# A retention and pooling block in split single precision: scores of 128 queries by one product of 256 columns, and keys, scores and states ahead of the filler

## The chip, the cores and the metric

The kernel runs on one core of a Trainium2 chip. Its time is the device time of one execution in microseconds (us). TensorE (PE in the profile) multiplies, VectorE (DVE) and ScalarE (ACT) do the elementwise work, SyncE (SP) issues the transfers, and GpSimd (POOL) does next to nothing here.

## What is computed

One layer on 1024 tokens of 1024 channels, float32: a gated feed-forward network (2816 wide), a mixing layer with two branches, retention in 4 heads of 256 and trailing mean pooling, and a second feed-forward network. The change lies in the mixing layer, in two places: where the values v are projected, and in the retention:

```python
def retention(q, k, v):
    ...
    scores = jnp.einsum("bnchd,bnshd->bnhcs", qc, kc) * inner_decay[None, None]
    inner = jnp.einsum("bnhcs,bnshe->bnche", scores, vc)

    def step(state, inp):
        q_i, k_i, v_i = inp
        cross = jnp.einsum("bchd,bhde->bche", q_i * q_decay[None, :, :, None], state)
        new_state = state * chunk_decay[None, :, None, None] + jnp.einsum(
            "bchd,bche->bhde", k_i * k_decay[None, :, :, None], v_i)
        return new_state, cross
    ...
    out = inner + cross.transpose(1, 0, 2, 3, 4)
```

## The kernel before

**Products in three parts.** Each float32 operand is split into a high part in the fast format fp32r and a low part, the rest: ACT casts (`copy`, line 161), DVE subtracts (`tt`, line 162; 165 and 166 with a scale). `mm3` (lines 178 to 183) adds three products in PSUM: high by high (181), high by low (182), low by high (183). So a product waits for ACT at line 181 and for DVE's low part at 182 or 183.

**Order of the work.** The kernel is a list of steps, each with a preparation (loads, splits) and a body (products). A helper called `flow` issues preparations four steps ahead of bodies and drains a queue of other work (`work`) in between. A scheduler then orders each engine's instructions statically, and `with soon():` gives instructions priority. PSUM has six rotating banks and two for sums.

**The values stage** (`values`, about 624 to 670 us in the profile). v = u W is one level of Strassen-Winograd's scheme: seven products of quarter blocks, L11 R11, S2 T2, S1 T1, S4 R22, S3 T3, L12 R21, L22 T4, each in four steps. L and S come from the weights (tiles vL, vS; their splits vL11w, vS1w, vS2w), R and T from the normalised activations (n2R, n2T). `block` builds the weight sums S2, S3 and S1 at lines 1271 to 1273. `nx.work` queues the work that makes an activation block; `end_of` does so as parts of the feed-forward network's sum are done: its `end(4)` queues R21 and T4. Just ahead of the values lies the end of that network: products bp6b of bp4m and bp4w, then the sums bd.

**The retention** (about 1153 to 1330 us). A `Unit` is half the sequence (512 tokens) of one head: 8 units, named by head and half (00, 01, 10 and so on). A unit has two spans of 256 tokens, each of two halves of 128. `scores` multiplies keys by queries: for the first 128 keys of a span against 256 queries (j = 0), for the second against 128 (j = 1), each over two halves of the head's 256 channels; DVE then scales by decay (tile sc) and the result is split (tile sm). `keys` transposes the keys (line 1434, PSUM tile kd00b and so on) and splits them with a scale (kd). `update` multiplies kd by v into a new state (PSUM tile st, tile sf, split into state). `across` multiplies queries by the state and `inner` the scores by v, both into ob. Units follow each other in `retention`; between their parts stand fillers, steps of the pooling branch (px) and of its projection (pu).

Of the kernel before, what the change touches and what calls it, by code (L numbers as in the profile page):

```python
# [15 lines left out]
ADD, SUB, MUL = ALU.add, ALU.subtract, ALU.mult  # L16

P = 128
# [27 lines left out]
SPAN = 2 * P  # L46
# [44 lines left out]
def block_kernel(ctx: ExitStack, tc, x, x_tok, vecs, f1_in, f1_out, w_in, w_v, pool_w, w_ret, w_pool, w_o,  # L91
                 f2_in, f2_out, g_row, rope, decay, consts, out, out_tok):
    nc = tc.nc
    mm = nc.tensor.matmul
# [84 lines left out]
    def mm3(dst, w, m, start, stop):  # L179

        mm(dst, w[0], m[0], start=start, stop=False, skip_group_check=True)  # L181
        mm(dst, w[0], m[1], start=False, stop=False, skip_group_check=True)  # L182
        mm(dst, w[1], m[0], start=False, stop=stop, skip_group_check=True)  # L183

    def parts(m, at=slice(None)):
        return m[:, 0, at], m[:, 1, at]
# [924 lines left out]

    mix = Next("n2", V_MIX, h1)

    def end_of(nx):
        def end(part):
            if part == 4:
                nx.work(nx.r21, nx.t4_)
            else:
                nx.work(*{2: (nx.r11,), 5: (nx.r22, nx.p22), 3: (nx.t2, nx.t1, nx.t3)}[part])

        return end

    end1 = end_of(mix)


    tab, stored = {}, set()
# [115 lines left out]
    def values():  # L1242

        nx, kept, two, p1s = mix, {}, {}, {}

        def fetch(r, *rows):

            for z, (k, o) in enumerate(rows):
                load(half(r, z), w_v[k, :, o * H : (o + 1) * H])
            return half(r, 0), half(r, 1)  # L1250

        def rows(n, k):

            if (n, k // 2) not in two:
                at, o = k // 2 * 2 + (4 if n[2] == "2" else 0), (1 if n[1] == "2" else 0)
                two[n, k // 2] = fetch(raw(f"v{n}{k}"), (at, o), (at + 1, o))
            return two[n, k // 2][k % 2]

        def block(n, k):

            if n[0] == "L":
                return rows(n, k)
            if n in ("S1", "S3"):
                return two.pop((n, k))

            L11 = rows("L11", k)
            if n == "S4":
                tt(L11, rows("L12", k), L11, SUB)
                return L11
            L21, L22 = fetch(tl(f"v{n}{k}"), (k, 1), (k + 4, 1))  # L1270
            tt(L22, L21, L22, ADD)
            tt(L21, L11, L21, SUB)
            tt(L11, L22, L11, SUB)
            two["S1", k], two["S3", k] = L22, L21
            return L11

        bk = {}

        def step(L, R, k, where, start, after):
            w = []  # L1280

            def prep():
                t = weights(block(L, k), f"v{L}w{k}")
                w.extend(flat(t, z) for z in range(2))

            def body():
                if start and k == 0:
                    for i in range(4):
                        bk[where, i] = (sum_bank if where == "b" and i < N_SUM else bank)(f"v{L}{i}")
                m = nx.operand(R, k)  # L1290
                for i in range(4):
                    mm3(bk[where, i], parts(m, slice(i * P, (i + 1) * P)), w, start and k == 0, k == 3)
                    if k == 3:
                        with soon():
                            after(i, bk[where, i])

            return prep, body

        def store(o, j, i, src):
            to = vs[2 * o + j].rearrange("p (h t c) -> p h t c", h=2, t=4)  # L1300
            load(to[:, :, i], src.rearrange("p (h c) -> p h c", h=2))
            if i == 3:
                stored.update(f"v{h}{j}" for h in (2 * o, 2 * o + 1))

        def keep(n, i):
            if i % 2 == 0:
                kept[n, i // 2] = t4(f"v{n}{i}")
            return half(kept[n, i // 2], i % 2)

        def old(n, i):  # L1310
            return half(kept[n, i // 2], i % 2)

        def result(o, j, other=None):
            def after(i, b):
                c = c2(f"vc{o}{j}{i}")
                if other is None:
                    copy(c, b)
                else:
                    tt(c, b, other(i), ADD)
                flow.add(lambda: store(o, j, i, c))  # L1320
                if (o, j, i) == (0, 0, 3):
                    nx.stats(between=nx.blocks("R22", [("tl", N_TL)] * 3, True))

            return after

        def after1(i, b):
            p1s[i] = c2(f"vp1{i}")
            copy(p1s[i], b)

        def after6(i, b):  # L1330
            copy(keep("h", i), b)

        def after5(i, b):
            copy(keep("f", i), b)

        def product(L, R, where, start, f):
            return [step(L, R, k, where, start, f) for k in range(4)]

        yield from product("L11", "R11", "a", True, after1)
        for p in zip(product("S2", "T2", "a", False, after6), product("S1", "T1", "b", True, after5)):  # L1340
            yield from p
        for p in zip(product("S4", "R22", "b", False, result(0, 1, lambda i: old("h", i))),
                     product("S3", "T3", "a", False, result(1, 1, lambda i: old("f", i)))):
            yield from p
        yield from product("L12", "R21", "b", True, result(0, 0, lambda i: p1s.pop(i)))
        yield from product("L22", "T4", "a", False, result(1, 0))
# [99 lines left out]
    class Unit:  # L1446
# [65 lines left out]
        def scores(self):  # L1512

            self.sm = []
            for j in range(2):
                wid = SPAN - j * P
                b = bank(f"s{self.name}{j}")
                for s in range(2):
                    at = s * SPAN + j * P
                    for i in range(2):  # L1520
                        mm3(b[:, s * wid : (s + 1) * wid], parts(self.K[i], slice(at, at + P)),
                            parts(self.Q[i], slice(at, at + wid)), s == 0 and i == 0, i == 1)
                n = 2 * wid
                c = c2(f"sc{self.name}{j}")
                m = sb.tile([P, 2, H], F32R, tag="t4", bufs=N_T4, name=f"sm{self.name}{j}")
                with soon():
                    for s in range(2):
                        at = slice(s * wid, (s + 1) * wid)
                        stt(c[:, at], b[:, at], self.row(8, 2 * s + j), self.dec[:, :wid], MUL, MUL)
                    split(m[:, 0, :n], m[:, 1, :n], c[:, :n])  # L1530
                self.sm.append(m)

# [41 lines left out]
        def across(self, s, state):  # L1574
            b, first = self.into(s)
            for t in range(2):
                at = s * SPAN + t * P
                for i in range(2):
                    mm3(self.cell(b, t), parts(self.Q[i], slice(at, at + P)),
                        parts(state, slice(i * HD, (i + 1) * HD)), first and i == 0 and t == 0, i == 1)  # L1580

        def products(self):
            self.ob = {}
            mid = self.update(0)
            if self.nh == 1:
                self.across(0, self.state)
            else:
                self.state = self.update(1)
            for s in range(2):
                self.inner(s)  # L1590
            self.across(1, mid)

        def outputs(self):
            o = self.O[self.nh] = t4(f"o{self.name}")
# [46 lines left out]
    def retention():  # L1641
        filler = fillers()

        def fill(n=1):
            for _ in range(n):
                f = next(filler, None)
                if f is not None:
                    yield f

        yield units[0].operands, units[0].values  # L1650
        for n, u in enumerate(units):
            after = units[n + 1] if n + 1 < len(units) else None

            def scores(u=u, n=n):
                if u.nh == 1:
                    u.follow(units[n - 1])
                u.scores()

            def rest(u=u, after=after):
                u.products()  # L1660
                if after:
                    after.operands()
                u.outputs()
                if u.nh == 1:
                    u.normalise()

            yield none, scores
            yield none, u.keys
            yield from fill()
            if after:  # L1670
                yield after.loads, lambda after=after: (after.values(), after.turn())
            yield none, rest

            late = u.nh == 0 and n
            if n < 3 or late:
                yield from fill()
            if late:
                yield none, units[n - 1].finish
        yield none, lambda: take(range(6))
        yield from fill(2)  # L1680
        yield none, units[-1].finish
        yield none, lambda: take((6, 7))
        yield from fill(2 * KT)
# [278 lines left out]
```

## Time and profile before

| | |
|---|---|
| median of 3 runs | 2150.41 us (2148.95 to 2151.13) |
| the profiled execution's own time | 2149.24 us |
| its span | 2147.2 us |
| PE busy, share of the span | 2134.6 us, 99% |
| DVE busy | 1871.7 us, 87% |
| ACT busy | 1100.8 us, 51% |

The span is the stretch that the profile shows; the other 2.04 us of the execution lie around it. In a timeline row stand the start, the length, the engine, the line, the operation, the output and the inputs, the shape (for PE the stationary operand, then the moving one), the number of instructions, and in brackets the idle time before it with what ended it. Matmuls are pipelined, so their lengths overlap: what a product takes is the distance from its start to the next one's. A row of the stretches names the busy time of each engine, with the number of its instructions.

### The profile page before, as it was taken

To read this page: it belongs to the slowest core of one execution; us is meant where nothing else is said; L and a number is where in the kernel's file an instruction comes from. 1 tells how busy PE (TensorE), PEld (TensorE's weight loads), DVE (VectorE), ACT (ScalarE), POOL (GpSimd) and SP (SyncE) were. 2 spreads that over 40 slices of the span, in tenths; PEclk is the share of its full clock that TensorE was granted. 3 is DMA by queue.
4 is the path that set the end of the run, shared out by engine and by line. 5 is a ranking of instruction groups with operands and counts; after the bars stand their busy time and mean duration, and the time that the engine had idled before them with its cause. 6 is when DMAs were issued, how large, how long until landed. Compare 5 with 4: busy or idle time off the path is not lost.

```text
span 2147.2 us, 30158 instructions
## 1 busy us (share of the span) xinstructions
PE 2134.6 (99%) x10830; PEld 1812.8 (84%) x10830; DVE 1871.7 (87%) x3344; ACT 1100.8 (51%) x2074; POOL 0.2 (0%) x4
## 2 busy tenths in 40 slices
PE   9999999999999999999999999999999999999998
PEld 7888888888887888888888888888888888888887
DVE  8798888997986799999988788899988988899796
ACT  8544444554653544545457653446644544455454
POOL 0000000000000000000000000000000000000000
PEclk9999999999999999999999999999999999999999
DMA  7232323585542333232337566624123232357542
GB/s 257 75 133 74 138 84 134 196 274 177 180 139 89 108 121 114 107 120 108 123 124 231 172 229 235 230 94 161 65 97 124 85 127 84 132 198 274 196 131 100
DMA packets 116102, 313.61 MB, mean 146 GB/s; under 512 B 12784, under 2 KB 17008, under 8 KB 115952
## 3 DMA queue, kind: packets, MB, share of 16 engines
q1 hardware_dynamic: 115376, 310.63, 41.9%
q8 instruction: 85, 1.39, 0.3%
q10 hardware_dynamic: 576, 1.05, 0.1%
q14 instruction: 65, 0.53, 0.1%
HBM read 220.93 MB, written 90.70 MB: 145 GB/s over the span
## 4 chain that ended last, share of the span: by engine, by line
PE 93%; DVE 4%; DMA 1%; ACT 1%; issue 0%; SPq 0%; DVEq 0%; ACTq 0%
PE c_b L181 2%; PE c_b L182 2%; PE c_b L183 2%; PE a_b L181 2%; PE a_b L182 2%; PE a_b L183 2%; PE c_e L181 2%; PE c_e L182 2%; PE c_e L183 2%; PE a_e L182 2%; PE a_e L181 2%; PE a_e L183 2%; PE a_a L181 1%; PE a_a L182 1%; PE a_a L183 1%; PE c_a L182 1%
## 5 line engine op out<-in xcount | busy, mean ns | idle before, releaser
L182 PE MATMUL c_b<-n3T,c_wS 128*128 128x512 f32 x176 | 68.6, 390 | 0.0
L183 PE MATMUL c_b<-n3T,c_wS 128*128 128x512 f32 x176 | 68.5, 389 | 0.0
L181 PE MATMUL c_b<-n3T,c_wS 128*128 128x512 f32 x176 | 68.2, 390 | 0.0
L181 PE MATMUL a_b<-n1T,a_wS 128*128 128x512 f32 x168 | 65.4, 389 | 0.0
L182 PE MATMUL a_b<-n1T,a_wS 128*128 128x512 f32 x168 | 65.4, 389 | 0.0
L183 PE MATMUL a_b<-n1T,a_wS 128*128 128x512 f32 x168 | 65.3, 389 | 0.0
L181 PE MATMUL a_a<-n1R,a_wL 128*128 128x512 f32 x120 | 46.7, 389 | 0.0
L182 PE MATMUL a_a<-n1R,a_wL 128*128 128x512 f32 x120 | 46.7, 389 | 0.0
L183 PE MATMUL a_a<-n1R,a_wL 128*128 128x512 f32 x120 | 46.7, 389 | 0.0
L182 PE MATMUL c_a<-n3R,c_wL 128*128 128x512 f32 x112 | 43.7, 390 | 0.0
L181 PE MATMUL c_a<-n3R,c_wL 128*128 128x512 f32 x112 | 43.6, 389 | 0.0
L183 PE MATMUL c_a<-n3R,c_wL 128*128 128x512 f32 x112 | 43.6, 389 | 0.0
L183 PEld LDWEIGHTS c_b<-n3T,c_wS 128*128 128x128 f32 x176 | 33.0, 188 | 6.9
L181 PEld LDWEIGHTS c_b<-n3T,c_wS 128*128 128x128 f32 x176 | 33.0, 188 | 6.7
L182 PEld LDWEIGHTS c_b<-n3T,c_wS 128*128 128x128 f32 x176 | 33.0, 188 | 6.6
L162 DVE TENSOR_TENSOR a_wS<-a_S,a_wS 128x512 fp32r<-128x512 f32 x45 | 30.6, 682 | 8.2 <-ACT a_wS L161 8.2
L183 PEld LDWEIGHTS a_b<-n1T,a_wS 128*128 128x128 f32 x168 | 31.5, 188 | 6.6
L181 PEld LDWEIGHTS a_b<-n1T,a_wS 128*128 128x128 f32 x168 | 31.5, 188 | 6.5
L182 PEld LDWEIGHTS a_b<-n1T,a_wS 128*128 128x128 f32 x168 | 31.5, 188 | 6.4
L162 DVE TENSOR_TENSOR c_wS<-c_S,c_wS 128x512 fp32r<-128x512 f32 x46 | 31.3, 682 | 3.7 <-ACT c_wS L161 3.6
L182 PE MATMUL c_e<-n3T,c_wL 128*128 128x512 f32 x88 | 34.5, 392 | 0.0
L181 PE MATMUL c_e<-n3T,c_wL 128*128 128x512 f32 x88 | 34.5, 392 | 0.0
(3378 smaller groups left out, 8145.1 us busy)
## 6 DMA issues: line engine op xcount, KB each, us to landing
c_ra<-in_f_in SPq DMA_DIRECT2D x22, 512.0 KB, 3.7
c_rb<-in_f_in SPq DMA_DIRECT2D x22, 512.0 KB, 3.7
a_ra<-in_f_in SPq DMA_DIRECT2D x21, 512.0 KB, 3.7
a_rb<-in_f_in SPq DMA_DIRECT2D x21, 512.0 KB, 3.7
t<-au SPq DMA_DIRECT2D x11, 512.0 KB, 2.9
b<-ag SPq DMA_DIRECT2D x11, 512.0 KB, 4.1
r<-au SPq DMA_DIRECT2D x11, 512.0 KB, 3.7
bra<-in_f_out SPq DMA_DIRECT2D x11, 512.0 KB, 5.5
```

The source lines that it names most:

```text
L162: tt(lo, src, hi.bitcast(F32), SUB)
L181: mm(dst, w[0], m[0], start=start, stop=False, skip_group_check=True)
L182: mm(dst, w[0], m[1], start=False, stop=False, skip_group_check=True)
L183: mm(dst, w[1], m[0], start=False, stop=stop, skip_group_check=True)
```

## The change

There are four edits. In the scores for j = 1, the high part of the keys is multiplied by the high and the low part of the queries side by side, one product of 256 columns into two halves of a PSUM strip; the low part of the keys by the high part of the queries is added to the first half. ACT copies the second halves out, DVE adds the first, and the decay is applied to that sum. In `retention`, keys come first, then scores, then the states (`updates`), and the filler after them; before it was scores, keys, filler, and the states after that, with the rest. R21 and T4 are queued from `values` at the third pair of steps of S2 T2 and S1 T1. The weight sums of `block` get priority.

```diff
-    def end_of(nx):
-        def end(part):
-            if part == 4:
-                nx.work(nx.r21, nx.t4_)
-            else:
-                nx.work(*{2: (nx.r11,), 5: (nx.r22, nx.p22), 3: (nx.t2, nx.t1, nx.t3)}[part])
-
-        return end
-
-    end1 = end_of(mix)
+    def end1(part):
+        mix.work(*{2: (mix.r11,), 5: (mix.r22, mix.p22), 3: (mix.t2, mix.t1, mix.t3)}.get(part, ()))
...
-            tt(L22, L21, L22, ADD)
-            tt(L21, L11, L21, SUB)
-            tt(L11, L22, L11, SUB)
+            with soon():
+                tt(L22, L21, L22, ADD)
+                tt(L21, L11, L21, SUB)
+                tt(L11, L22, L11, SUB)
...
-        for p in zip(product("S2", "T2", "a", False, after6), product("S1", "T1", "b", True, after5)):
+        for k, p in enumerate(zip(product("S2", "T2", "a", False, after6), product("S1", "T1", "b", True, after5))):
+            if k == 2:
+                nx.work(nx.r21, nx.t4_)
             yield from p
...
-                    at = s * SPAN + j * P
+                    at, to = s * SPAN + j * P, b[:, s * SPAN : (s + 1) * SPAN]
                     for i in range(2):
-                        mm3(b[:, s * wid : (s + 1) * wid], parts(self.K[i], slice(at, at + P)),
-                            parts(self.Q[i], slice(at, at + wid)), s == 0 and i == 0, i == 1)
+                        w, m = parts(self.K[i], slice(at, at + P)), self.Q[i][:, :, at : at + wid]
+                        first, final = s == 0 and i == 0, i == 1
+                        if j == 0:
+                            mm3(to, w, (m[:, 0], m[:, 1]), first, final)
+                        else:
+                            mm(to, w[0], m, start=first, stop=False, skip_group_check=True)
+                            mm(to[:, :P], w[1], m[:, 0], start=False, stop=final, skip_group_check=True)
...
                 with soon():
+                    src = b
+                    if j:
+                        both, src = b.rearrange("p (s z c) -> p s z c", s=2, z=2), c
+                        sums = c[:, :n].rearrange("p (s c) -> p s c", s=2)
+                        copy(sums, both[:, :, 1])
+                        tt(sums, both[:, :, 0], sums, ADD)
                     for s in range(2):
                         at = slice(s * wid, (s + 1) * wid)
-                        stt(c[:, at], b[:, at], self.row(8, 2 * s + j), self.dec[:, :wid], MUL, MUL)
+                        stt(c[:, at], src[:, at], self.row(8, 2 * s + j), self.dec[:, :wid], MUL, MUL)
...
+        def updates(self):
+
+            self.mid = self.update(0)
+            if self.nh == 0:
+                self.state = self.update(1)
+
         def products(self):
             self.ob = {}
-            mid = self.update(0)
             if self.nh == 1:
                 self.across(0, self.state)
-            else:
-                self.state = self.update(1)
             for s in range(2):
                 self.inner(s)
-            self.across(1, mid)
+            self.across(1, self.mid)
...
-            yield none, scores
-            yield none, u.keys
+            yield none, keys
+            yield none, u.scores
+            yield none, u.updates
             yield from fill()
```

The order of the instructions moves in the two stages alone. On DVE, at the end of the feed-forward network, these rows follow each other before; vL11w_5938 is the first weight block of the values, bd the sum that ends the network:

```order
L162 TENSOR_TENSOR bp4w_5909<-bL_5879,bp4w_5909 128x512 [waits DMAHW6_49,PE_49]
L162 TENSOR_TENSOR bp4m_5912<-bT_5882,bp4m_5912 128x512 [waits DMAHW0_49,Activation_49]
L318 SCALAR_TENSOR_TENSOR bacc_4359<-bacc_4359,neg,bacc_4363 128x512 [waits DMAHW1_49]
L318 SCALAR_TENSOR_TENSOR bacc_4360<-bacc_4360,neg,bacc_4364 128x512 [waits DMAHW2_49]
L162 TENSOR_TENSOR vL11w_5938<-vL_5935,vL11w_5938 128x512 [waits DMAHW7_49,Activation_49]
L162 TENSOR_TENSOR n2T_5928<-bacc_4359,n2T_5928 128x512 [waits Activation_49]
L162 TENSOR_TENSOR n2T_5932<-bacc_4360,n2T_5932 128x512 [waits Activation_49]
L318 SCALAR_TENSOR_TENSOR bacc_4361<-bacc_4361,neg,bacc_4365 128x512 [waits DMAHW3_49]
L953 TENSOR_TENSOR bd_6000<-bp6b_4193,brb 128x512 [waits PE_49]
```

In the changed kernel the same place on DVE, from bp4m_5912 on, reads:

```order
L162 TENSOR_TENSOR bp4m_5912<-bT_5882,bp4m_5912 128x512 [waits Activation_49]
L318 SCALAR_TENSOR_TENSOR bacc_4359<-bacc_4359,neg,bacc_4363 128x512
L318 SCALAR_TENSOR_TENSOR bacc_4360<-bacc_4360,neg,bacc_4364 128x512
L953 TENSOR_TENSOR bd_6000<-bp6b_4193,brb 128x512 [waits PE_49]
L953 TENSOR_TENSOR bd_6005<-bp6b_4194,brb 128x512 [waits PE_49]
L953 TENSOR_TENSOR bd_6010<-bp6b_4195,brb 128x512 [waits PE_49]
L953 TENSOR_TENSOR bd_6015<-bp6b_4196,brb 128x512 [waits PE_49]
L1264 TENSOR_TENSOR vS_6173<-vS_6173 128x512 [waits DMAHW6_49,DMAHW5_49,DVE_49]
L162 TENSOR_TENSOR n2T_5928<-bacc_4359,n2T_5928 128x512 [waits Activation_49]
L1265 TENSOR_TENSOR vS_6173<-vL_5976,vS_6173 128x512 [waits DVE_49]
L162 TENSOR_TENSOR n2T_5932<-bacc_4360,n2T_5932 128x512 [waits Activation_49]
L162 TENSOR_TENSOR vL11w_5938<-vL_5935,vL11w_5938 128x512
```

The low part of vL11w_5938 stood three places behind that of bp4m_5912 and ahead of bd; now it stands eleven places behind it, after bd and two weight sums (lines 1264 and 1265). Four more of these sums now stand ahead of bp4m_5912, two of them as far up as the earlier bd.

On PE, in the retention's unit 20, the scores of 128 queries (PSUM tile s_11945) end before like this, and the transposes of the keys and a filler (pu1d) follow:

```order
L183 MATMUL s_11945<-q_11883,k_11889 128x128
L181 MATMUL s_11945<-q_11886,k_11892 128x128
L182 MATMUL s_11945<-q_11886,k_11892 128x128
L183 MATMUL s_11945<-q_11886,k_11892 128x128
L1434 MATMUL kd20b_11969<-cst,k_11687 128x128 [waits DMAHW3_49,PE_49]
L1434 MATMUL kd20b_11969<-cst,k_11687 128x128 [waits DMAHW4_49]
L1434 MATMUL kd20b_11969<-cst,k_11687 128x128 x2
L1434 MATMUL kd20b_11979<-cst,k_11687 128x128 x4
L700 MATMUL pu1d_11771<-po_11269,pu1w_11797 128x512
```

In the changed kernel the transposes stand ahead of all scores, and the same place reads:

```order
L1521 MATMUL s_11957<-q_11867,k_11873 128x256 [waits PE_49]
L1522 MATMUL s_11957<-q_11867,k_11873 128x128
L1521 MATMUL s_11957<-q_11870,k_11876 128x256
L1522 MATMUL s_11957<-q_11870,k_11876 128x128
L1521 MATMUL s_11957<-q_11867,k_11873 128x256
L1522 MATMUL s_11957<-q_11867,k_11873 128x128
L1521 MATMUL s_11957<-q_11870,k_11876 128x256
L1522 MATMUL s_11957<-q_11870,k_11876 128x128
L181 MATMUL st_11979<-v_11807,kd_11919 128x256 [waits Activation_49]
L182 MATMUL st_11979<-v_11807,kd_11919 128x256
L183 MATMUL st_11979<-v_11807,kd_11919 128x256 [waits DVE_49]
```

Where twelve products of 128 columns stood, there are four of 256 and four of 128, and the state's products (st) follow at once, with waits for ACT and DVE on kd. Before, 24 filler products stood between the transposes and the first of them.

On DVE, in unit 00, the low part of the first keys (k_10809) stands before in this place; the rows at 1153, 1160 and 589 belong to the projections that end there:

```order
L1153 TENSOR_TENSOR g2A<-g2b,g2A 128x512 [waits DVE_49,PE_49]
L162 TENSOR_TENSOR q_10806<-q_10556,q_10806 128x512
L1160 TENSOR_TENSOR g2A<-g2A,n2rb 128x512 [waits DVE_49]
L162 TENSOR_TENSOR k_10809<-k_10559,k_10809 128x512 [waits DMAHW0_49]
L1153 TENSOR_TENSOR g3B<-g3e,g3v 128x512 [waits PE_49]
```

In the changed kernel:

```order
L1145 TENSOR_TENSOR g2A<-g2b,g2A 128x512 [waits DVE_49,PE_49]
L166 SCALAR_TENSOR_TENSOR kd_10915<-kd00b_10914,by_10901,kd_10915 128x256 [waits Activation_49]
L1152 TENSOR_TENSOR g2A<-g2A,n2rb 128x512 [waits DVE_49]
L166 SCALAR_TENSOR_TENSOR kd_10915<-kd00b_10914,by_10901,kd_10915 128x256 [waits Activation_49]
L162 TENSOR_TENSOR q_10806<-q_10556,q_10806 128x512
L1145 TENSOR_TENSOR g3B<-g3e,g3v 128x512 [waits PE_49]
L589 TENSOR_TENSOR g3A<-g2x_10815,g3A 128x256 [waits Activation_49]
L1152 TENSOR_TENSOR g3B<-g3B,n2rb 128x512 [waits DVE_49]
L166 SCALAR_TENSOR_TENSOR kd_10925<-kd00b_10924,by_10901,kd_10925 128x256 [waits Activation_49]
L1145 TENSOR_TENSOR g3A<-g3b,g3A 128x512 [waits DVE_49]
L162 TENSOR_TENSOR k_10809<-k_10559,k_10809 128x512 [waits DMAHW0_49]
```

The keys' low part moved behind three kd splits and four steps of the projections.

More of the change, by code (lines that the diff above doesn't have):

```diff
@@ L1652, in retention, with keys @@
             after = units[n + 1] if n + 1 < len(units) else None
-            def scores(u=u, n=n):
+            def keys(u=u, n=n):
                 if u.nh == 1:
                     u.follow(units[n - 1])
-                u.scores()
+                u.keys()
             def rest(u=u, after=after):
```

## The prediction

> **What bounds the kernel now.** I read the page's first and fourth parts, then the waits of the tensor engine, then the groups by shape and the timelines of the two stages that the change touches.
>
> ```profile
> PE 2134.6 (99%) x10830; PEld 1812.8 (84%) x10830; DVE 1871.7 (87%) x3344; ACT 1100.8 (51%) x2074; POOL 0.2 (0%) x4
> PE 93%; DVE 4%; DMA 1%; ACT 1%; issue 0%; SPq 0%; DVEq 0%; ACTq 0%
> ```
>
> The tensor engine (PE) is busy for 2134.6 of the span's 2147.2 us, and the chain that ended last is PE for 93% of its length. So the time changes by what PE no longer has to do, and by waits of PE that come or go. All its waits are few:
>
> ```profile
> engine line waited for: us in total, times, longest us
> PE vL L181 <- ACT vS2w L161: 1.5, 1, 1.5
> PE set L204 <- DVE zero L199: 1.2, 1, 1.2
> PE ob L182 <- DVE state L162: 1.1, 2, 0.8
> PE ob L181 <- ACT state L161: 0.6, 2, 0.5
> ```
>
> The 1.2 us is the start of the kernel and stays. The change can touch the other three: one stall of 1.5 us in the values stage, and 1.1 + 0.6 = 1.7 us in which the retention waits for its state. Whatever else it gains must be PE work that vanishes.
>
> **Scores of 128 queries.** Each of the 8 retention units has 2 spans and 2 key halves, so 32 groups; each group was three products of 128 columns and becomes one of 256 and one of 128. The durations of single products overlap, so I price them by the distance between starts, in one stretch of the stage:
>
> ```profile
> 1283.60 0.28 PE L181 MATMUL s<-q,k 128*128 128x256 f32 x1
> ...
> 1284.31 0.23 PE L181 MATMUL s<-q,k 128*128 128x128 f32 x1
> 1284.37 0.27 PE L182 MATMUL s<-q,k 128*128 128x128 f32 x1
> ...
> 1285.15 0.28 PE L183 MATMUL s<-q,k 128*128 128x128 f32 x1
> ```
>
> From 1283.60 to 1284.31 lie six products of 256: 0.118 us each. From 1284.37 to 1285.15 lie seven of 128: 0.111 each. Half as many columns are hardly cheaper: a group costs 3 x 0.111 = 0.333 before and 0.118 + 0.111 = 0.229 after, 0.104 less, and 32 x 0.104 = 3.3 us less PE work. The new operand reads the high and the low part of the queries as two strips of 128. No row shows a product of two strips; its bounds are 0.118 (one strip of 256, above) and 0.222 (two products of 128). I take 0.118, since the rest of the instruction is that row's; at 0.222 the whole 3.3 is gone.
>
> [...]
>
> Off PE each unit gains an ACT copy and a DVE addition of 256 elements:
>
> ```profile
> L162 DVE TENSOR_TENSOR sm<-sc,sm 128x256 fp32r<-128x256 f32 x8 | 3.3, 416 | 0.2
> L161 ACT CAST sm<-sc 128x256 fp32r<-128x256 f32 x8 | 3.3, 407 | 6.5 <-DVE sc L1529 6.3
> ```
>
> That is 8 x 0.41 = 3.3 us on each. What is late by it are the parts of the 128-query scores, by 0.8 us, which the inner products read only after the states and the filler (in unit 20, below, the filler runs from 1245 past 1249.49). I cost it at nothing. Without that cover it would be 8 x 0.8 = 6.4 us.
>
> **States ahead of the filler.** The state products now follow the scores at once, so the state is split while the filler runs, several us before the cross products that read it. The 1.7 us of state waits go. In exchange the kd operands (keys transposed, scaled by ACT and DVE) are needed without the filler between. In the unit 20 of before:
>
> ```profile
> 1244.26 1.06 PE L1434 MATMUL kd20b<-cst,k 128*128 128x128 f32 x8
> 1247.56 0.48 DVE L166 SCALAR_TENSOR_TENSOR kd<-kd20b,by,kd 128x256 fp32r<-128x256 f32 x1
> 1249.13 0.47 DVE L166 SCALAR_TENSOR_TENSOR kd<-kd20b,by,kd 128x256 fp32r<-128x256 f32 x1
> 1249.49 0.39 PE L701 MATMUL pu1d<-po,pu1w 128*128 128x512 f32 x1
> ```
>
> Its transposes end at 1245.32; the second low part is done at 1248.04, 2.7 us later, the fourth at 1249.60, 4.3 later. Between transposes and states now stand 12 x 0.118 + 4 x 0.229 = 2.3 us of scores; the second low part is read 5 products (0.6) into the states, the fourth 17 products (2.0) in: 2.7 against 2.9 and 4.3 against 4.3. So it just fits where ACT and DVE are as free as here, and they are not everywhere:
>
> ```profile
> core 0: us, PE busy (x) PEld busy (x) DVE busy (x) ACT busy (x) POOL busy (x), PEclk, DMA share, GB/s
> 1150.00:1180.00 30.00, 29.84 (x198) 27.03 (x197) 29.85 (x56) 25.04 (x52) 0.00 (x0) 1.00 0.72 232
> 1270.00:1300.00 30.00, 29.52 (x194) 26.61 (x193) 29.89 (x64) 16.35 (x41) 0.00 (x0) 1.00 0.37 128
> ```
>
> DVE is full from 1150 to 1180, where unit 00 starts, and around unit 30, whose keys it rotates first. In unit 00 three kd splits, and four steps of the sums that stood behind, now come ahead of the first keys' low part:
>
> ```profile
> 1158.46 0.68 DVE L162 TENSOR_TENSOR k<-k,k 128x512 fp32r<-128x512 f32 x1
> 1159.06 0.68 DVE L1153 TENSOR_TENSOR g3B<-g3e,g3v 128x512 f32<-128x512 f32 x1
> ...
> 1164.30 0.86 DVE L166 SCALAR_TENSOR_TENSOR kd<-kd00b,by,kd 128x256 fp32r<-128x256 f32 x2
> 1159.67 0.28 PE L183 MATMUL s<-q,k 128*128 128x256 f32 x1
> ```
>
> Three splits at 0.4 (a pair takes 0.86), three steps of 0.6 (1158.46 to 1159.06) and one of half that make it 3.3 us later: done at 1158.46 + 3.3 + 0.68 = 1162.4. PE is given six pool products of 0.23 (the distance of starts at 512 columns, below) and eight transposes of 0.11 ahead of the score product of 1159.67, 2.3 us, and is there at 1162.0: a wait of 0.4. The second keys' low part follows 1.6 later, behind a split and a step, and PE has 1.1 us of work until it: 0.5 more. That is 0.9, between nothing and 3.3. For the other seven units I take 0.7 together (unit 30 and unit 10, whose kd splits stand behind the casts of values and queries), between nothing and 1.15 each (a pair of casts, below). Retention in sum: -3.3 - 1.7 + 0.9 + 0.7 = -3.4. SP's queue moves too: unit 20's q and k loads stand behind some result writes. None of PE's waits ends on a load, and I put nothing for it.
>
> **The values stage.** The work for the operands R21 and T4 is queued later, and three sums over weight rows are pulled ahead by priority. The stall that they can free:
>
> ```profile
> 653.06 0.39 PE L183 MATMUL vS<-vS1w,n2T 128*128 128x512 f32 x1
> 654.93 1.20 PE L181 MATMUL vL<-vS2w,n2T 128*128 128x512 f32 x4 [1.48 <-ACT vS2w L161]
> 631.30 0.39 PE L181 MATMUL vL<-vL11w,n2R 128*128 128x512 f32 x1
> 631.53 0.39 PE L182 MATMUL vL<-vL11w,n2R 128*128 128x512 f32 x1
> ```
>
> Products of 512 start 0.23 apart, so the gap of 1.87 costs 1.64 us. It goes: the sum that vS2w waits for is one of those pulled ahead. But DVE has no idle time here (16.00 of 16 us, first row), so what is put ahead makes something else late:
>
> ```profile
> 624.00:640.00 16.00, 16.00 (x72) 13.15 (x72) 16.00 (x27) 7.40 (x14) 0.00 (x0) 1.00 0.31 110
> 602.96 0.81 SPq L140 DMA_DIRECT2D vL<-in_w_v  x2
> vL<-in_w_v SPq DMA_DIRECT2D x8, 256.0 KB, 3.0
> 605.24 1.28 DVE L967 TENSOR_TENSOR bacc<-bacc,bd 128x512 f32<-128x512 f32 x2
> 625.80 0.68 DVE L162 TENSOR_TENSOR bp4m<-bT,bp4m 128x512 fp32r<-128x512 f32 x1
> 627.73 0.68 DVE L162 TENSOR_TENSOR vL11w<-vL,vL11w 128x512 fp32r<-128x512 f32 x1
> 630.20 2.48 DVE L953 TENSOR_TENSOR bd<-bp6b,brb 128x512 f32<-128x512 f32 x4
> 628.58 0.39 PE L181 MATMUL bp6b<-bp4m,bp4w 128*128 128x512 f32 x1
> 628.81 0.39 PE L182 MATMUL bp6b<-bp4m,bp4w 128*128 128x512 f32 x1
> ```
>
> DVE reaches the first pulled-up sum at 605.24, but its rows, issued at 602.96 with 3.0 to landing, are there at 605.96: 0.7 lost. Four sums at 0.6 (starts at DVE are 0.60 apart) then stand ahead of bp4m's low part: 2.4 + 0.7 = 3.1 later, done at 625.80 + 3.1 + 0.68 = 629.6, where PE wants it at 628.81: a stall of 0.8. Next in the old order came vL11w's low part at 627.73; in the new one it stands behind the four bd sums, two more weight sums and two n2T splits. The bd sums need the last PE product of bp6b and end by 633.2; four steps of 0.6 follow, so vL11w is done at 633.2 + 2.4 + 0.7 = 636.3. PE, with four high products put ahead, wants it at 631.30 + 0.8 + 4 x 0.23 = 633.0: a stall of 3.3. Behind it DVE's next low parts (one every 0.6 to 2.4 us) serve 2.7 us of PE work each, so no further stall. Sum: 0.8 + 3.3 - 1.64 = +2.5. Bounds: -1.6 if PE finds vL11w in time, +4.0 if the last weight rows land late (0.6) and the second split is late as well (0.7).
>
> **Sum.** -3.4 + 2.5 = -0.9 us against the profiled execution's 2149.24 (span 2147.2 and 2.04 around it): 2148.3. The median shown, 2150.41, is 1.2 above that execution, so 2149.5 is forecast. A measurement of this kernel can tell about 0.2%, 4.3 us, from no change; the forecast lies within it.
>
> **The rivals.**
> *Faster: the values stage does not stall.* If DVE's order costs PE nothing there, all that remains is -3.4 - 1.6 = -5.0, and 2145.4; with no new kd waits -6.6 and 2143.8, the most that the change can bring. For it: the old stall ends on ACT, which has slack, and the early stalls rest on times that I chained over 30 us of DVE. Against: the order of DVE is fixed, and no gap in it was there to absorb 3.1 us. Chance 0.28.
>
> *Slower: states wait for kd.* The state products have lost their cover. If in each unit the kd splits stand behind one pair of casts, PE waits for it eight times:
>
> ```profile
> 1248.92 1.15 ACT L161 CAST q<-q 128x512 fp32r<-128x512 f32 x2
> ```
>
> 8 x 1.15 = 9.2 in place of my 0.7 gives -0.9 + 8.5 = +7.6, 2158.0. It decides from a wait of (4.3 + 0.9 + 0.7) / 8 = 0.75 us a unit. For it: 2.7 against 2.9 leaves no margin, and in unit 20 that pair of casts does stand right beside the kd splits. Against: ACT has half its time free, and the kd splits are now released ahead of the scores' parts, not behind them. Chance 0.19.
>
> *The cheap product is not cheap.* Two strips of 128 cost 0.222 as two products do: the 3.3 us are not won, and the sum is +2.4, 2152.8, still within what counts as the same. [...] Against: the seven rows at 0.111. Chance 0.05.
>
> **How the numbers follow.** The forecast has 0.48. Faster by over 0.2% has 0.28, from the first rival; within 0.2% has 0.48 + 0.05 = 0.53; slower 0.19. The range leaves out the corner of the first rival with no new wait at all, and the upper part of the second: 2144.5 to 2155.0.
>
> **What would show it.** Right: s products of 256 columns in place of 192 of the small ones, their starts 0.12 apart; no PE wait on state; the vL wait on vS2w gone; and a new PE wait on vL11w's low part of about 3 us and one on bp4m's of under 1. Wrong: no wait on vL11w (then faster), waits of the st products on kd in most units (then slower), or two-strip products 0.2 apart.

## The result, and the profile after

The changed kernel is slower: 2156.24 us median against 2150.41, a ratio of 1.0028 (95% interval 1.0017 to 1.0039). The forecast was 2149.5, in a range from 2144.5 to 2155.0. Its profiled execution took 2154.68 us with a span of 2151.8.

The first line of its page's busy times, then the waits of PE that bear on the change. The numbers of a wait are us in total, how often, and the longest:

```profile
PE 2133.0 (99%) x10798; PEld 1810.7 (84%) x10798; DVE 1874.5 (87%) x3352; ACT 1103.4 (51%) x2082; POOL 0.2 (0%) x4
```

```profile
PE vL L182 <- DVE vL11w L162: 4.3, 1, 4.3
PE st L181 <- ACT kd L165: 1.6, 3, 1.1
...
PE bp6b L182 <- DVE bp4m L162: 1.2, 1, 1.2
...
PE vS L182 <- DVE vS1w L162: 0.7, 1, 0.7
...
PE px L181 <- DVE g3A L1145: 0.5, 1, 0.5
...
PE s L183 <- DVE k L162: 0.3, 1, 0.3
```

The waits on vS2w (1.5) and on state (1.7) are gone, as forecast. New ones stand in their place, the largest on vL11w.

Where the time went is read from marks that both kernels share: starts of products before the change's places, between them and after. These are rows of the tiles' view, of before and then of after; the numbers behind the colon are lengths in ns, then the first and last start.

```profile
L181 PE MATMUL bp6b<-bp6m,bp6w x44: 389/389/389, 424.6 to 481.0; 128*128 128x512 f32 x44
L181 PE MATMUL q0a<-n2R,q0wL x8: 389/389/389, 711.3 to 718.8; 128*128 128x512 f32 x8
L181 PE MATMUL g3b<-n2T,g3wS x8: 389/389/389, 1135.7 to 1143.1; 128*128 128x512 f32 x8
L181 PE MATMUL ru0a<-ruR,ru0wL x8: 389/389/389, 1358.6 to 1366.1; 128*128 128x512 f32 x8
```

```profile
L181 PE MATMUL bp6b<-bp6m,bp6w x44: 389/389/390, 424.8 to 481.2; 128*128 128x512 f32 x44
L181 PE MATMUL q0a<-n2R,q0wL x8: 389/390/390, 718.2 to 725.7; 128*128 128x512 f32 x8
L181 PE MATMUL g3b<-n2T,g3wS x8: 389/390/390, 1142.3 to 1149.8; 128*128 128x512 f32 x8
L181 PE MATMUL ru0a<-ruR,ru0wL x8: 389/389/390, 1363.3 to 1370.8; 128*128 128x512 f32 x8
```

From bp6b to q0a, the stretch of the values stage, 286.7 us became 293.4: 6.7 lost, where +2.5 was forecast. From the last g3b to the first ru0a, the retention, 215.5 became 213.5: 2.0 won, where 3.4 was forecast. Together that is 4.7, and the span grew by 4.6. The time outside the span grew by 0.8 (from 2.0 to 2.9), for which no row shows a reason.

PE in the values stage of after:

```profile
628.76 0.39 PE L181 MATMUL bp6b<-bp4m,bp4w 128*128 128x512 f32 x1
630.31 0.50 PE L182 MATMUL bp6b<-bp4m,bp4w 128*128 128x512 f32 x1 [1.16 <-DVE bp4m L162]
...
632.96 1.07 PE L181 MATMUL vL<-vL11w,n2R 128*128 128x512 f32 x4
638.35 0.50 PE L182 MATMUL vL<-vL11w,n2R 128*128 128x512 f32 x1 [4.33 <-DVE vL11w L162]
...
639.74 0.63 PE L182 MATMUL vL<-vL11w,n2R 128*128 128x512 f32 x1
640.17 0.63 PE L183 MATMUL vL<-vL11w,n2R 128*128 128x512 f32 x1
...
650.55 0.61 PE L181 MATMUL vS<-vS1w,n2T 128*128 128x512 f32 x2
651.82 0.50 PE L182 MATMUL vS<-vS1w,n2T 128*128 128x512 f32 x1 [0.66 <-DVE vS1w L162]
```

Behind the long wait the products start 0.43 us apart (639.74 to 640.17), not 0.23. The stretches show why. They are cut at 638.95 and 642.36, where the clock changes; in each row the granted clock (PEclk in the head) stands behind the engines, ahead of the DMA's share.

```profile
core 0: us, PE busy (x) PEld busy (x) DVE busy (x) ACT busy (x) POOL busy (x), PEclk, DMA share, GB/s
635.54:638.95 3.41, 0.60 (x3) 0.51 (x4) 3.41 (x7) 0.00 (x0) 0.00 (x0) 1.00 0.01 2
638.95:642.36 3.41, 3.41 (x10) 2.65 (x9) 3.41 (x7) 1.86 (x4) 0.00 (x0) 0.50 0.00 0
642.36:645.78 3.42, 3.42 (x16) 2.80 (x15) 3.42 (x7) 0.95 (x2) 0.00 (x0) 1.00 0.00 0
```

The clock stood at 0.5 for 3.4 us with PE busy throughout, which loses half of that, 1.7. By the distances of the starts, the stretch's loss adds up: 1.55 - 0.23 = 1.3 at bp4m, 638.35 - 632.96 - 4 x 0.23 = 4.5 at vL11w, 1.7 by the clock, 651.82 - 650.55 - 2 x 0.23 = 0.8 at vS1w, less the old 1.64: 6.7.

DVE in the same stretch of after:

```profile
627.76 0.69 DVE L1264 TENSOR_TENSOR vS<-vS 128x512 f32<-128x512 f32 x1 [0.67 <-DMA vS<-in_w_v]
...
631.50 2.48 DVE L953 TENSOR_TENSOR bd<-bp6b,brb 128x512 f32<-128x512 f32 x4
635.20 0.69 DVE L1264 TENSOR_TENSOR vS<-vS 128x512 f32<-128x512 f32 x1 [1.23 <-DMA vS<-in_w_v]
...
637.61 0.68 DVE L162 TENSOR_TENSOR vL11w<-vL,vL11w 128x512 fp32r<-128x512 f32 x1
```

DVE stood 1.23 us for the rows of the fourth weight block, with vL11w's low part four places behind it: PE stood still behind a weight sum that its own products need only later.

### The profile page after: what moved, and what is told of

Its sections match the earlier page's. It is cut to its first block, busy times and chain, and to the rows that moved or that the text cites. A ratio compares the mean times of both kernels' runs of the same rounds, so it can differ in the third digit from the quotient of the medians.

```text
span 2151.8 us, 30116 instructions
## 1 busy us (share of the span) xinstructions
PE 2133.0 (99%) x10798; PEld 1810.7 (84%) x10798; DVE 1874.5 (87%) x3352; ACT 1103.4 (51%) x2082; POOL 0.2 (0%) x4
## 4 chain that ended last, share of the span: by engine, by line
PE 87%; DVE 8%; DMA 2%; ACT 2%; issue 1%; SPq 0%; DVEq 0%; ACTq 0%
PE c_b L181 2%; PE c_b L182 2%; PE c_b L183 2%; PE a_b L181 2%; PE a_b L182 2%; PE a_b L183 2%; PE c_e L181 2%; PE c_e L182 2%; PE c_e L183 2%; PE a_e L182 2%; PE a_e L181 2%; PE a_e L183 2%; PE a_a L181 1%; PE a_a L182 1%; PE a_a L183 1%; PE c_a L182 1%
```

## The experiments

Times are medians; each ratio is to runs of the kernel before on the same chip, whose median was 2149.53 to 2150.41 us. The stretches are read as above, in the one profiled execution of each kernel.

| kernel | us | ratio to before (95%) | values | retention |
|---|---|---|---|---|
| before | 2150.41 | | 286.7 | 215.5 |
| changed | 2156.24 | 1.0028 (1.0017 to 1.0039) | 293.4 | 213.5 |
| values_undone | 2148.48 | 0.9994 (0.9985 to 1.0003) | 286.7 | 214.4 |
| no_soon | 2146.18 | 0.9987 (0.9978 to 0.9995) | 285.0 | 213.1 |
| soon3 | 2151.62 | 1.0009 (1.0000 to 1.0018) | 289.0 | 214.0 |
| filled | 2155.87 | 1.0025 (1.0015 to 1.0035) | 291.8 | 215.9 |
| scores_only | 2146.11 | 0.9983 (0.9974 to 0.9992) | 286.8 | 211.6 |
| order_only | 2153.02 | 1.0018 (1.0009 to 1.0027) | 286.8 | 218.8 |
| scores_late | 2143.18 | 0.9973 (0.9961 to 0.9984) | 285.0 | 212.1 |
| pw_soon | 2146.26 | 0.9984 (0.9975 to 0.9993) | 285.0 | 213.5 |
| late_states_after_fill | 2151.13 | 1.0005 (0.9997 to 1.0014) | 284.9 | 216.2 |
| soon_only_queue_old | 2156.86 | 1.0030 (1.0017 to 1.0042) | 294.4 | 214.7 |
| late_scores_first | 2147.01 | 0.9986 (0.9977 to 0.9995) | 285.0 | 214.0 |

**Which stage loses.** values_undone is the changed kernel with the priority and the late queue taken back:

```diff
-            with soon():
-                tt(L22, L21, L22, ADD)
...
+            tt(L22, L21, L22, ADD)
...
-            if k == 2:
-                nx.work(nx.r21, nx.t4_)
```

> The changed kernel with the two values-stage edits taken back (no priority for the weight sums, R21 and T4 queued as before); scores and retention order stay changed. Theory: the whole loss lies in the values stage (its end, the first q0a product, is 6.7 us late in the changed kernel) and the retention gained 2.0 (the delay shrinks from 6.7 to 4.7 by the first ru0a product). So 2.0 us faster than the kernel before, about 2148.4, with the 1.5 us wait on vS2w back and no wait on vL11w. Rival: the retention edits lose and only look like a gain since they start late; then it is no faster than 2150.4.

The values stretch is back at 286.7, and the kernel is 1.2 us faster than before beside it (2149.65), though the interval reaches no change. So the net loss comes from the two edits of the values stage; what the other two won and lost is parted further below.

**Which of its two edits.** no_soon takes back the priority only, the first diff; soon_only_queue_old takes back only the late queue (R21 and T4 queued from `values`), the second.

```diff
-            with soon():
-                tt(L22, L21, L22, ADD)
...
+            tt(L22, L21, L22, ADD)
```

```diff
+            if part == 4:
+                nx.work(nx.r21, nx.t4_)
...
-            if k == 2:
-                nx.work(nx.r21, nx.t4_)
```

> The changed kernel without the priority of the weight sums; R21 and T4 stay queued late. Theory: the priority alone puts the sums ahead of vL11w's low part, so the waits on bp4m, vL11w and vS1w go; the late queue takes four splits off DVE before 654 us, so the old wait on vS2w goes too: 2.0 + 1.6 = 3.6 us faster than before, about 2146.8. Rival: moving R21 and T4 is what reorders DVE; then the wait on vL11w stays and the time is about that of the changed kernel, 2156.

> The changed kernel with R21 and T4 queued as before; the priority of the weight sums stays. Theory: the priority alone makes the loss; the DVE rows from bp4m to vL11w are the same as in the changed kernel, so the wait of 4.3 us on vL11w, the half-speed products and the wait on bp4m stay, 2156 or up to 1 more, since the splits of R21 and T4 are back in the full stretch of DVE. Rival: late queue and priority make it only together; then the wait on vL11w is under 2 us and the time under 2151.

Without the priority the stretch is 285.0, 1.7 shorter than before: the late queue alone removes the old stall and brings no new one. With the priority alone it is 294.4, with the same 4.3 us wait on vL11w. The whole times agree: 3.5 us below the kernel before beside it, and 6.8 above. The priority makes the whole loss.

**What in it.** soon3 gives the priority to three of the four weight blocks:

```diff
-            with soon():
+            with soon() if k < 3 else ExitStack():
```

> The changed kernel with the priority kept for the first three of the four weight blocks only, so the two sums of the fourth and their wait for rows (1.23 us) no longer stand ahead of vL11w's low part. Theory with the clock: PE's wait on vL11w falls from 4.3 by 1.2 + 1.2 to about 1.9 us, which is too short to lower the granted clock, so the 1.6 us of half-speed products go as well: 4.0 us less than the changed kernel, about 2152.2, products behind the wait 0.23 apart. Rival, waits only (the slow products come from DVE's traffic): 2.4 less, 2153.8, and products still 0.43 apart behind the wait.

The stretch shrinks by 4.4 us, 293.4 to 289.0. Its wait and its clock:

```profile
635.73 0.50 PE L182 MATMUL vL<-vL11w,n2R 128*128 128x512 f32 x1 [1.83 <-DVE vL11w L162]
```

```profile
632.22:635.63 3.41, 1.68 (x8) 1.07 (x6) 3.41 (x7) 0.00 (x0) 0.00 (x0) 1.00 0.36 124
635.63:639.05 3.42, 3.32 (x14) 2.58 (x15) 3.42 (x7) 2.36 (x4) 0.00 (x0) 1.00 0.00 0
```

The wait is 2.5 shorter and the clock stays at 1.0: two sums and one wait for rows were worth 2.5. The other 1.9 are the clock's 1.7 and shorter waits on bp4m (1.0) and vS1w (0.2), which this run does not part. The time, 2151.62, lies by the theory with the clock (2152.2), not by the waits alone (2153.8).

**The clock by itself.** filled leaves DVE as it is and gives PE something to do while it waits:

```diff
                 m = nx.operand(R, k)
+                if L == "L11" and k == 0:
+                    for _ in range(18):
+                        mm(bk[where, 3], m[:, 0, 3 * P :], w[0], start=True, stop=False, skip_group_check=True)
```

> The changed kernel with 18 extra products of 512 columns put into the wait on vL11w (the first high products repeated into a bank that is started anew afterwards, 18 x 0.23 = 4.1 us of PE work where it would stand idle). Theory: it is the idle time that lowers the granted clock; with PE busy the clock stays at 1.0, the products behind the wait are 0.23 apart instead of 0.43, and although the work is more, the time falls by 1.6 less 0.45 (two high products fewer are put ahead), 1.2 us less than the changed kernel, 2155.0. Rival: the slow products are slowed by other traffic at that place; then they stay 0.43 apart and the time is that of the changed kernel or 0.5 more.

```profile
632.44 4.24 PE L1286 MATMUL vL<-vL11w,n2R 128*128 128x512 f32 x18
...
637.75 0.50 PE L182 MATMUL vL<-vL11w,n2R 128*128 128x512 f32 x1 [0.61 <-DVE vL11w L162]
638.08 0.39 PE L183 MATMUL vL<-vL11w,n2R 128*128 128x512 f32 x1
638.31 0.40 PE L182 MATMUL vL<-vL11w,n2R 128*128 128x512 f32 x1
```

Products behind the wait start 0.23 apart, and the stretch is 1.6 us shorter than the changed kernel's, with 18 products more and DVE's order up to the wait unchanged. The clock, 0.50 for 3.4 us in the changed kernel, is 1.00 here in every stretch of 1 us from 630 to 650. So it was PE's idleness that lowered it there. But the whole time did not fall as expected: it lies 6.2 us above the kernel before beside it, the changed kernel's 5.8 above its own. In the profiled execution the retention gave the gain back, with a wait of 3.0 us for kd where the changed kernel had 1.1; why, is shown below.

**The retention, edit by edit.** Both are the kernel before with one part of the change: scores_only with the new scores, the first diff, order_only with the new order, the second.

```diff
...
+                            mm(to, w[0], m, start=first, stop=False, skip_group_check=True)
+                            mm(to[:, :P], w[1], m[:, 0], start=False, stop=final, skip_group_check=True)
...
+                        copy(sums, both[:, :, 1])
+                        tt(sums, both[:, :, 0], sums, ADD)
```

```diff
...
-            yield none, scores
-            yield none, u.keys
+            yield none, keys
+            yield none, u.scores
+            yield none, u.updates
             yield from fill()
```

> The kernel before with the new scores of 128 queries alone (old order in the retention, values stage as before). Theory: 32 groups of products cost 0.229 us instead of 0.333, so 3.3 us less PE work, and the added copy and addition lie behind the filler: 3.3 faster than before, about 2146.6, the stretch from the last g3b product to the first ru0a product 212.2 us instead of 215.5. Rival: the copy and addition delay the scores' split in units where DVE is full, and eat half or more: 2148.5 or later, with new waits of ob on sm.

> The kernel before with the new order in the retention alone (keys, scores, states, then filler; old scores, values stage as before). Theory: the 1.7 us of waits on state go, and waits of st on kd (1.6), of px on g3A (0.5) and on a key's low part (0.3) come: +0.7 us, about 2150.6, the stretch from g3b to ru0a about 216.2. Rival: with the old, longer scores between keys and states (1.0 us more in all of a unit's 20 groups' place) the kd splits are in time, and the order gains its 1.7: 2148.2, 213.8.

The scores win 3.4 us against 2149.53, as worked out. In the stretch it is 3.9, of which 0.7 are waits: where before waited 1.7 for state, this run waits 1.0 for k, v and state together. That leaves 3.2 for the products. The order alone loses 3.5, where 0.7 was expected and the rival had a gain; both missed. Two of its waits, and the clock behind them:

```profile
1185.41 0.39 PE L181 MATMUL st<-v,kd 128*128 128x256 f32 x1 [0.56 <-ACT kd L165]
...
1187.51 0.39 PE L183 MATMUL st<-v,kd 128*128 128x256 f32 x1 [1.60 <-DVE kd L166]
```

```profile
1185.38:1188.79 3.41, 1.78 (x7) 1.09 (x7) 3.20 (x8) 3.41 (x8) 0.00 (x0) 1.00 0.76 284
1188.79:1192.21 3.42, 3.36 (x13) 3.08 (x13) 2.16 (x5) 1.37 (x4) 0.00 (x0) 0.50 0.34 95
```

Again 3.4 us at half clock, 1.7 lost.

**Why kd is late.** In the runs with the new order, ACT stands at the cast of the pooling weights (pw) until their load lands, and then works almost without a gap up to the late kd. pw_soon is no_soon with priority for that load:

```diff
-            load(half(r, 0), pool_w[n])
+            with soon():
+                load(half(r, 0), pool_w[n])
```

> The changed kernel without the priority of the weight sums, and with priority for the load of the pooling weights pw, which puts it one place further ahead in SP's queue (ahead of the write of g3A that waits for ACT). Theory: the wait of st on kd01 comes from ACT standing 0.7 to 3.3 us at the cast of pw until its load lands; 2.2 us earlier in the queue that wait goes and with it the 0.9 us of st's: 0.9 less than without (2145.3). Rival: kd01 is late by ACT's own work (casts of pl, scaling of po) and the time stays at 2146.2.

```profile
1167.64 0.62 ACT L161 CAST pw<-pw 128x512 fp32r<-128x512 f32 x1 [2.49 <-DMA pw<-in_pool_w]
...
1180.45 2.41 ACT L165 ACTIVATE po<-px,vec 128x512 fp32r<-128x512 f32 x4
1182.74 0.48 ACT L165 ACTIVATE kd<-kd01b,by 128x256 fp32r<-128x256 f32 x1
```

The time stayed at 2146.26, as the rival said. But the run does not tell whether the load makes kd late. It was issued only 0.7 us earlier (1163.06 for 1163.80), 0.4 of which is the whole execution's lead, and not 2.2; and ACT's cast moved ahead of two others, so that ACT stood there 2.49 us where it stood 0.69 in no_soon.

The other traces show that it does. Here is ACT's wait for the load and PE's first wait for kd, in the changed kernel and then in filled:

```profile
1177.67 0.62 ACT L161 CAST pw<-pw 128x512 fp32r<-128x512 f32 x1 [1.41 <-DMA pw<-in_pool_w]
1192.10 0.39 PE L181 MATMUL st<-v,kd 128*128 128x256 f32 x1 [1.06 <-ACT kd L165]
```

```profile
1177.72 0.62 ACT L161 CAST pw<-pw 128x512 fp32r<-128x512 f32 x1 [3.32 <-DMA pw<-in_pool_w]
1192.15 0.39 PE L181 MATMUL st<-v,kd 128*128 128x256 f32 x1 [2.98 <-ACT kd L165]
```

In the six kernels with the new order and scores and no priority for this load (no_soon, soon3, the changed one, values_undone, soon_only_queue_old, filled), it took 4.7, 5.4, 5.4, 5.7, 6.3 and 7.4 us from issue to landing. ACT waited 0.69, 1.40, 1.41, 1.66, 2.23 and 3.32 us for it, and PE 0.35, 1.06, 1.06, 1.33, 1.90 and 2.98 for kd: 0.33 to 0.35 less each time. So the landing of this one load sets the longest wait on kd in this order. Why it takes longer in one execution than in another is not shown.

**Which half of the order.** Two variants of no_soon: states behind the filler with keys first, and states ahead of it with scores first.

```diff
             yield none, u.scores
-            yield none, u.updates
             yield from fill()
+            yield none, u.updates
```

> The changed kernel without the priority of the weight sums, and with the states one place later: keys, scores, filler, states (the changed kernel has keys, scores, states, filler; before it was scores, keys, filler, states). Theory: what the new order loses is the filler's cover of the kd splits; with it back the waits of st on kd go (0.9 to 1.4 us in the runs without priority, all before 1207 us), and the time is that of new scores with late queue and the old order, 2143.2 to 2144. Rival: it is the keys ahead of the scores that cost (kd splits ahead of the keys' low parts on DVE, waits of px on g3A and of s on k, 0.8 us); then about 2145.5, with the waits of px and s still there.

```diff
                     u.follow(units[n - 1])
-                u.keys()
+                u.scores()
...
-            yield none, u.scores
+            yield none, u.keys
             yield none, u.updates
             yield from fill()
```

> New scores, late queue, no priority, and in the retention scores, keys, states, filler: the states ahead of the filler as in the changed kernel, but the keys behind the scores as before. It parts the two halves of the new order. Theory A, the states' lost cover is the cost: between keys and states nothing is left (before: filler; changed: 2.3 us of scores), so st waits for kd 1 to 2 us in several of the eight units, and the time is 3 us or more above the 2146.2 of the variant with keys first, 2149 or later. Theory B, the keys ahead of the scores are the cost (the rotation in units 30 and 31 and the keys' low parts are wanted earlier): then kd waits stay near 1.5 us in all and the time falls toward the 2143.2 of the old order.

The first misses its forecast and its rival's: kd's waits went, but others came, on the rotation of the keys in units 30 and 31 (kd30b and kd31b) among them, and one behind the retention lowered the clock.

```profile
PE ru1b L181 <- ACT ru1wS L161: 2.1, 1, 2.1
PE s L183 <- DVE k L162: 1.6, 3, 0.7
PE kd31b L1428 <- DVE k L1477: 1.4, 1, 1.4
```

```profile
1370.08:1373.49 3.41, 1.44 (x7) 0.86 (x5) 2.04 (x4) 0.57 (x2) 0.00 (x0) 1.00 1.02 389
1373.49:1380.32 6.83, 6.50 (x14) 4.62 (x15) 6.05 (x10) 2.72 (x6) 0.00 (x0) 0.50 0.86 285
```

Here the clock was low for 6.8 us. This execution, with 2153.64 us, was the slowest of eleven (2147.91 to 2153.64), so the median of 2151.13 need not hold that drop. The second, without any scores between keys and states, waits for kd only 0.8 us in all and ends at 2147.0, so neither of its theories holds. Against scores_late below, which keeps the old order, the first loses 7.4 us, the second 3.4, and both halves together (no_soon) 2.9, each time measured from the kernel before beside it. The halves do not add up, their waits move from place to place, and the first puts the states ahead of the next unit's values, which the old order did not; so their prices are not parted.

**The best version.** scores_late is scores_only with the late queue.

```diff
-            if part == 4:
-                nx.work(nx.r21, nx.t4_)
...
+            if k == 2:
+                nx.work(nx.r21, nx.t4_)
```

> The kernel before with the new scores and with R21 and T4 queued late (no priority, old order in the retention). Theory: 3.3 from the scores and 1.6 from the values stage, where the late queue alone already gave 1.7 in the trace without priority: 4.9 faster than before, about 2145.0, and no slower than the variant without priority but with the new order (3.5 faster). Rival: the new order is worth its 1.7 and this is 1.7 slower than that variant.

It beats both kernels: 2143.18 us, 6.4 below before beside it, where the changed kernel is 5.8 above. That is 1.4 more than the two gains were expected to give. With the new order in its place (no_soon) it was 2146.18; the new order won nothing, so the rival is out, though the two intervals overlap. PE's largest wait after the start is now 0.5 us in two parts, on state.

## Why the prediction was wrong, point by point

- **The new scores: right.** 3.4 us measured for 3.3, of which the products won 3.2 in the stretch; that the whole came out so near is in part luck, since waits changed beside it. The two strips cost no more here than one: in after, a product of 256 starts 0.17 us ahead of the next, one of 128 only 0.06, 0.23 a pair where 0.229 was worked out. So the sign "starts 0.12 apart" holds for the pair's mean alone; and the small products replaced are 96 (12 in each of 8 units), not 192. The rival of the dear strips fell.

```profile
1289.99 0.34 PE L1521 MATMUL s<-q,k 128*128 128x256 f32 x1
1290.16 0.23 PE L1522 MATMUL s<-q,k 128*128 128x128 f32 x1
1290.22 0.33 PE L1521 MATMUL s<-q,k 128*128 128x256 f32 x1
```

- **The values stage: right in mechanism, wrong in size.** Of the 6.4 us by which the profiled execution missed its 2148.3, 4.2 lie in this stretch, 1.4 in the retention and 0.8 outside the span. The failing step is "a stall of 3.3" at vL11w, and what was taken to follow it. The wait itself cost 4.5, since the last weight rows landed 1.23 us late; the prediction had that as a bound of 0.6. The bp4m stall cost 1.3 for 0.8, with 0.67 of wait for rows ahead of it. "So no further stall" missed vS1w (0.8). And 1.7 us have no term in the sum at all: the clock, which filled shows to come from PE's idleness. The upper bound of +4.0, which its own terms make 3.8, was passed by 2.7.
- **States ahead of the filler: the sum's 0.9 + 0.7 for new waits was too small.** The waits of after are 1.6 + 0.5 + 0.3 = 2.4, which with -3.3 and -1.7 makes -2.6; the stretch shows -2.0, and 0.6 has no wait to go with it. The 1.7 of state waits was no price of the old order: with the new scores and the old order 0.2 (scores_only) and 0.5 us (scores_late) of them are left. "None of PE's waits ends on a load, and I put nothing for it" failed too: the longest wait on kd ends on ACT, and ACT had stood behind the load of pw. The order, costed at about nothing, loses 2.3 us even with the new scores (values_undone against scores_only, each against the kernel before beside it); only that kd wait of 1.3 us has a cause shown.
- **The rivals.** The faster one fell with the wait on vL11w. The slower one named the wrong place: states waited for kd three times, 1.6 us in all, not in eight units for 1.15 each. The true price on the slow side, a wait that also halves the clock, was not among them.

## What to carry to other kernels

Before giving work priority on an engine that is full, list what it is put ahead of and when each of those is wanted; and whether its own inputs have landed, since a wait in a queue is passed to all behind it: here DVE's 1.23 us for rows, to vL11w four places behind. Price a long stall of PE by more than its length: here a drop of the clock to 0.5 for 3.4 us added 1.7, or, by estimate, about twice that when it lasted 6.8 (PE was busy for 6.50 of them). An edit of several parts is best run part by part: two parts of this one are worth 6.4 us, and with the other two the kernel is 12 us slower than with those alone.

## What the runs showed of the hardware that was not expected

The low clock came in lengths of 3.4 us (after, order_only) and 6.8 (late_states_after_fill, soon_only_queue_old). It followed PE waits of 4.3 us, of 0.6 and 1.6 close together, and of 2.1. It did not follow one of 1.8 (soon3), nor the one of 3.0 in filled:

```profile
1190.30:1193.71 3.41, 1.56 (x8) 1.29 (x8) 3.41 (x7) 3.41 (x8) 0.00 (x0) 1.00 0.91 331
1193.71:1197.12 3.41, 3.25 (x19) 2.50 (x18) 2.84 (x8) 3.41 (x8) 0.00 (x0) 1.00 0.20 66
```

So here the length of a wait alone did not decide it.

In the four traces in which the clock fell and recovered ahead of the end, the moments at which it changes lie whole steps of 3.413 us apart, read from the mean clock of short stretches. In after it recovers at 642.36 and falls next at 2147.64, behind the last product, and 1505.28 / 441 = 3.4133. In order_only it is 955.73 / 280 (1192.21 to 2147.94), in late_states_after_fill 768.00 / 225 (1380.32 to 2148.32) and in soon_only_queue_old 1508.70 / 442 (644.00 to 2152.70), each 3.4133; the low lengths of 3.4 and 6.8 us are one and two of them. Counted back in these steps from the last fall of each trace, the clock fell behind steps at full clock in which the stretches count few products (3 in after, 7 in order_only and late_states_after_fill), and not behind two with 8 (filled from 1190.30; soon3 from 632.22, a row that starts 0.07 us behind its step). In filled the wait of 3.0 us, from 1189.17 to 1192.15, was split between two steps. So in these traces where a wait fell against the steps counted as well as its length. The cases are few and their products differ in width, so what makes the clock fall is not shown beyond them.
